# LayerNorm in a two-layer backbone: the norm's output from the centred residual in two VectorE operations a tile, the residual's own normalisation as a third one later, and the Newton step on VectorE

## The chip, the cores and the metric

The kernel runs on one core of one Trainium2 chip. The metric is the device time of one execution in microseconds (us). Before the change the median of three runs is 1936.71 us. A core has five engines that each work through a queue of their own in order: TensorE (PE, matrix products), VectorE (DVE), ScalarE (ACT), GpSimd (POOL) and SyncE (SP, which issues most transfers). They wait for each other by semaphores.

## The reference, cut to what matters

The reference is a backbone of two layers over 256 latent tokens and 256 context tokens, 1024 features each, in float32. Each layer has three sublayers: a SwiGLU, a mixer (an mLSTM in the first layer, windowed attention in the second) and another SwiGLU. Each is followed by a LayerNorm of the scaled residual, and its input is that residual, modulated by coefficients from a conditioning vector:

```python
def layer_norm(x, g, b):
    mu = xf.mean(-1, keepdims=True)
    var = jnp.mean(jnp.square(xf - mu), -1, keepdims=True)
    return ((xf - mu) * lax.rsqrt(var + LN_EPS) * g + b)

def modulate(s, m, slot):
    return s * (1 + m[..., 3 * slot + 1, :]) + m[..., 3 * slot, :]

def residual_post_norm(s, y, gate, weight, g, b):
    return layer_norm(ALPHA * s + weight * gate * y, g, b)
```

Between two sublayers the kernel needs two results of a norm: `u`, the modulated input of the next sublayer (soon), and `ALPHA` times the normalised residual, to which the next sublayer's output is added (late).

## The kernel before

The residual lies feature-major in eight tiles `as_[d]` of 128 features by 512 tokens. Columns `C0` (0 to 255) are the context, `C1` (256 to 511) the latent tokens. A matrix product in float32 is made of three products of halves: each operand is split into a rounded high part and a low part, the rest. Weights come by DMA into `raw` tiles; ScalarE writes the high part (L384), VectorE the low part as raw minus high (L385, L1298 for the attention's weights). One matmul of 128x128 by 256 columns follows the other at about 0.12 us.

A hand-written planner emits the program: tasks are generators with priorities, a clock `k.T` counts TensorE's time, and each `yield` says how much of that time is to pass before a task goes on. TensorE's and SyncE's orders are the planner's own; the orders of VectorE, ScalarE and GpSimd come from a scheduler with priorities.

`class Norm` makes one norm. There are five between the sublayers: into the mLSTM, after it, after the first layer's last SwiGLU, into attention, and after attention. The first four work on two halves, `C0` first and then `C1`; the fifth on `C1` alone (`solo`). (A sixth, `Last`, writes the output and is another class.) The steps of a norm:

- `__init__`: a per-token shift is taken off the residual on GpSimd (L88).
- `add`: when a sublayer's output `y` for tile d has been added (L787, VectorE, reads PSUM), sums of the residual and of its square are accumulated (L107, L108) on VectorE or GpSimd.
- `finish(cs)`, once for each half, nine times in all: small matmuls (`stat`) sum over the features. ScalarE squares the mean (L138) and copies the mean square plus `EPS` (L139), GpSimd subtracts (L140). `rsqrt` is a power on GpSimd (L820) and a Newton step of four operations on GpSimd (L822 to L825), all on 128x2 values `ln`. GpSimd then takes the mean off eight tiles (L145). Matmuls spread `rstd` over 128 partitions into a PSUM tile.
- Then, for each tile: VectorE multiplies the tile by `rstd` (L168), ScalarE makes the high part `uh` = tile x A + B (L581), VectorE the same in full as `uf` (L582) and the low part `ul` = `uf` - `uh` (L583). The solo norm writes both parts into one tile `up`. Head matmuls of the next sublayer (`xm`, `gv`, `k`, `v`) read `uh` and `ul` tile by tile.
- After a yield of `RY`, GpSimd scales the tile for the residual, times `ALPHA` g plus `ALPHA` b (L174).

Of the kernel before, what the change touches and what calls it, by code (L numbers as in the profile page):

```python
# [8 lines left out]
F32 = mybir.dt.float32  # L9
# [4 lines left out]
AF = mybir.ActivationFunctionType  # L14
ALU = mybir.AluOpType
# [7 lines left out]
EPS = 1e-5  # L23
# [49 lines left out]
class Norm:  # L73
# [44 lines left out]
    def finish(s, cs):  # L118
        k, nc = s.k, s.k.nc
        P = nc.gpsimd  # L120
        k.res[cs.start] = Ev()
        yield 0 if s.solo else LAT[0] if cs == s.halves[0] else LAT[1]

        st = k.ps("stat")
        o = 256 - cs.start
        parts = [(s.a1[:, cs], s.a2[:, cs])]
        if s.solo:

            parts.append((k.as_[KD - 1][:, cs], s.sq[:, cs]))
        for i, p in enumerate(parts):  # L130
            for n in range(2):
                s.moments(st, o, p[n], n, i == n == 0)
        for i, p in enumerate(parts):
            k.mm(st[:, cs], k.ones[1024], p[0], False, i == len(parts) - 1)
        mu = s.a1
        w = [k.sp.tile([128, 2], F32, tag=f"ln{n}", name="ln", bufs=2) for n in range(4)]
        with k.tc.high_priority(offset=400):
            nc.scalar.activation(w[0], st[:, o:o + 2], AF.Square)  # L138
            nc.scalar.activation(w[1], st[:, o + 2:o + 4], AF.Copy, bias=EPS)  # L139
            P.tensor_tensor(out=w[1], in0=w[1], in1=w[0], op=ALU.subtract)  # L140
            y = k.rsqrt(w[1], w[2], w[3], True)
        nc.scalar.activation(mu[:, cs], st[:, cs], AF.Copy)
        for d in range(KD):
            r = k.as_[d][:, cs]
            k.tc.keep_in_program_order(P.tensor_tensor(out=r, in0=r, in1=mu[:, cs], op=ALU.subtract))  # L145
        if s.solo:
            k.free(s.sq)
        s.left -= 1
        if s.left == 0:
            k.calm.t = k.T + CALM  # L150
        if s.left == 0:
            k.free(s.a1, s.a2)
        if s.solo:
            k.keep_warm(WARM[0])
        yield SOLO if s.solo else LAT[2]
        bc = k.ps("rstd")
        for t in range(2):
            k.mm(bc[:, cs.start + 128 * t:cs.start + 128 * t + 128], y[:, t:t + 1].to_broadcast([128, 128]), k.ident, t == 0, True)
        if s.solo:
            k.keep_warm(WARM[1])  # L160
        c = 0 if cs == C1 else 1
        s.ready[cs.start].t = k.T + (LAT[3] if cs == s.halves[0] else LAT[4])
        y = bc[:, cs]
        if s.u is None:
            s.u = k.new_u(s.solo)
        for d in range(KD):
            r = k.as_[d][:, cs]
            nc.vector.tensor_tensor(out=r, in0=r, in1=y, op=ALU.mult)  # L168
            A, B = s.AB
            k.modulate(r, A[:, d, c:c + 1], B[:, d, c:c + 1], cs, s.u[d])  # L170
        yield RY
        for d in range(KD):
            r = k.as_[d][:, cs]
            nc.gpsimd.tensor_scalar(out=r, in0=r, scalar1=s.ag[:, 0, d:d + 1], scalar2=s.ag[:, 1, d:d + 1], op0=ALU.mult, op1=ALU.add)  # L174
        k.res[cs.start].t = k.T


# [1405 lines left out]
```

## Time and profile before

| | |
|---|---|
| Runs, us | 1936.71, 1938.23, 1934.01 (median 1936.71) |
| The profiled execution, us | 1940.04, its span 1938.0 |
| Mean granted TensorE clock | 0.983 |
| TensorE busy | 1884.1 us, 97% of the span |
| VectorE busy | 1355.2 us, 70% |
| ScalarE busy | 835.0 us, 43% |
| GpSimd busy | 365.8 us, 19% |

The times in the profile's rows are from the start of the span. In a row, the first number is the start, the second the duration, then engine, line and operation, what it writes and reads, how many instructions the row merges, and in brackets how long the engine had been idle and what ended that. The busy share of TensorE says that most of the kernel cannot be moved by other engines; the places where TensorE waits for one are short and known by name. The clock in a stretch is the share of TensorE's full speed that was granted there.

### The profile page before, as it was taken

What the parts mean: (1) busy time and instruction counts of PE and PEld (TensorE: products, weight loads), DVE (VectorE), ACT (ScalarE), POOL (GpSimd) and SP (SyncE); (2) the same over time, 40 slices, a digit from 0 to 9 for tenths busy, and PEclk for the clock granted to TensorE, in tenths of its full rate; (3) what the DMA queues carried; (4) which work ended last, traced back from release to release, by engine and by line L of the source; (5) the groups of instructions that cost most, each with busy time, mean ns of one, the idle gap of its engine ahead of it and who ended that gap; (6) DMA issues with size and microseconds to landing.
All of it is one profiled execution on the core that took longest, in us unless ns stands there. A gap on an engine that the chain in (4) does not pass through costs nothing.

```text
span 1938.0 us, 28054 instructions
## 1 busy us (share of the span) xinstructions
PE 1884.1 (97%) x10498; PEld 1594.5 (82%) x10498; DVE 1355.2 (70%) x2476; ACT 835.0 (43%) x1565; POOL 365.8 (19%) x397
## 2 busy tenths in 40 slices
PE   7999999999999999989999999999999999989997
PEld 4888888897889977978888889888888898788887
DVE  4976677976664679767776679876733468967675
ACT  3443233246555563343323333433223335747562
POOL 2000000570012344450000015400000256130000
PEclk9999999999999999989999999999999999989999
DMA  9654454435343364325454444354422324125653
GB/s 317 218 202 167 152 192 161 136 121 184 96 150 115 129 220 141 109 93 185 153 200 174 158 136 142 127 199 152 153 89 91 103 73 131 45 66 172 210 174 98
DMA packets 227432, 287.49 MB, mean 148 GB/s; under 512 B 7968, under 2 KB 197536, under 8 KB 227296
## 3 DMA queue, kind: packets, MB, share of 16 engines
q1 hardware_dynamic: 226384, 282.75, 44.0%
q0 software_dynamic: 912, 2.95, 0.4%
q8 instruction: 82, 1.34, 0.3%
q14 instruction: 54, 0.44, 0.1%
HBM read 269.94 MB, written 15.73 MB: 147 GB/s over the span
## 4 chain that ended last, share of the span: by engine, by line
PE 56%; DVE 3%; POOL 1%; issue 1%; ACT 0%; DVEq 0%; POOLq 0%; ACTq 0%
PE gv L294 31%; PE y L294 19%; PE q L294 1%; PE o L294 1%; PE s L294 1%; DVE ul L583 1%; PE stat L294 1%; DVE uf L582 0%; PE pT L301 0%; PE msum L294 0%; PE h L294 0%; POOL as L145 0%; DVE as L168 0%; ACT e L1412 0%; PE swap L294 0%
## 5 line engine op out<-in xcount | busy, mean ns | idle before, releaser
L294 PE MATMUL gv<-uh,w 128*128 128x512 f32 (+1 forms) x2240 | 673.1, 381 | 11.0 <-DVE w L385 5.5
L384 ACT ACTIVATE w<-raw 128x512 fp32r<-128x512 f32 x636 | 395.9, 630 | 667.0 <-PE gv L294 373.8
L385 DVE TENSOR_TENSOR w<-raw,w 128x512 fp32r<-128x512 f32 x604 | 433.3, 724 | 278.5 <-ACT w L384 275.4
L294 PEld LDWEIGHTS gv<-uh,w 128*128 128x128 f32 x2240 | 417.3, 191 | 97.3 <-DVE w L385 5.7
L294 PE MATMUL gv<-ul,w 128*128 128x512 f32 (+1 forms) x1120 | 425.3, 380 | 0.1
L502 DVE SCALAR_TENSOR_TENSOR macc<-mraw,cs,macc 128x512 f32<-128x512 f32 x448 | 330.9, 784 | 44.4 <-DMA mraw<-in_mod_w 32.8
L294 PE MATMUL y<-hh,w 128*128 128x512 f32 (+1 forms) x1248 | 341.1, 359 | 0.0
L294 PEld LDWEIGHTS y<-hh,w 128*128 128x128 f32 x1248 | 222.6, 189 | 37.8 <-issue 3.2
L294 PEld LDWEIGHTS gv<-ul,w 128*128 128x128 f32 x1120 | 213.5, 191 | 38.6 <-DVE ul L583 0.6
L88 POOL TENSOR_TENSOR as<-as,shift 128x512 f32<-128x512 f32 (+1 forms) x40 | 57.6, 1475 | 889.6 <-ACT shift L86 889.6
L294 PE MATMUL y<-hl,w 128*128 128x512 f32 (+1 forms) x624 | 222.4, 356 | 0.0
L294 PEld LDWEIGHTS y<-hl,w 128*128 128x128 f32 x624 | 117.9, 189 | 17.5 <-issue 0.7
L294 PE MATMUL gv<-up,w 128*128 128x512 f32 x704 | 125.1, 340 | 2.0 <-DVE up L583 2.0
L294 PEld LDWEIGHTS gv<-up,w 128*128 128x128 f32 x704 | 109.8, 192 | 17.2 <-DVE up L583 2.3
L787 DVE SCALAR_TENSOR_TENSOR as<-y,gate,as 128x256 f32<-128x256 f32 x192 | 82.0, 476 | 34.6 <-PE y L294 34.5
L294 PE MATMUL z<-w,uh 128*128 128x256 f32 x512 | 94.1, 285 | 0.0
L294 PE MATMUL xm<-uh,w 128*128 128x512 f32 (+1 forms) x320 | 91.7, 360 | 0.0
L294 PE MATMUL y<-hnh,w 128*128 128x512 f32 (+1 forms) x320 | 85.2, 350 | 1.4 <-DVE as L787 1.4
L385 POOL TENSOR_TENSOR w<-raw,w 128x512 fp32r<-128x512 f32 x32 | 46.4, 1452 | 201.0 <-ACT w L384 194.5
L294 PEld LDWEIGHTS z<-w,uh 128*128 128x128 f32 x512 | 79.8, 191 | 2.5 <-issue 2.1
L700 DVE TENSOR_TENSOR sg<-sg,gv 128x512 f32<-128x512 f32 x66 | 44.9, 685 | 48.9 <-PE gv L294 47.5
L294 PE MATMUL z<-w,ul 128*128 128x256 f32 x256 | 72.4, 283 | 0.0
(309 smaller groups left out, 2541.3 us busy)
## 6 DMA issues: line engine op xcount, KB each, us to landing
raw<-in_ffn_w_in SPq DMA_DIRECT2D x84, 1024.0 KB, 5.2
mraw<-in_mod_w SPq DMA_DIRECT2D x128, 512.0 KB, 6.2
raw<-in_ffn_w_out SPq DMA_DIRECT2D x48, 768.0 KB, 4.6
raw<-in_ml_w_up SPq DMA_DIRECT2D x15, 1024.0 KB, 5.7
m<-in_mod_w SPq DMA_DIRECT2D x32, 256.0 KB, 6.6
raw<-in_ffn_w_out SPq DMA_DIRECT2D x16, 512.0 KB, 3.5
raw<-in_ml_w_down SPq DMA_DIRECT2D x16, 512.0 KB, 4.0
raw<-in_at_w_qkv SPq DMA_DIRECT2D x6, 1024.0 KB, 5.1
```

What stands on the lines that cost most here:

```text
L88: nc.gpsimd.tensor_tensor(out=k.as_[d][:, cols], in0=k.as_[d][:, cols], in1=sh[:, cols], op=ALU.subtract)
L294: k.nc.tensor.matmul(out, lhsT=lhsT, rhs=rhs, start=start, stop=stop, skip_group_check=True, **kw)
L384: k.nc.scalar.activation(h, view, AF.Copy)
L385: (k.nc.gpsimd if pool else k.nc.vector).tensor_tensor(out=l, in0=view, in1=h.bitcast(F32), op=ALU.subtract)
L502: V.scalar_tensor_tensor(out=o, in0=r, scalar=cf, in1=o, op0=ALU.mult, op1=ALU.add)
L583: nc.vector.tensor_tensor(out=lo, in0=f[:, cs], in1=hi.bitcast(F32), op=ALU.subtract)
L700: nc.vector.tensor_tensor(out=sg[:, cols], in0=sg[:, cols], in1=gv[1][:, cols], op=ALU.mult)
L787: nc.vector.scalar_tensor_tensor(out=k.as_[d][:, cs], in0=ys[dp][e][:, part], scalar=G[:, d, c:c + 1], in1=k.as_[d][:, cs], op0=ALU.mult, ...
```

## The change

The variance is now one VectorE operation from the statistics in PSUM and ScalarE's square (L141). The power stays on GpSimd (L143). The Newton step is three operations on VectorE (L144 to L146). The mean is still taken off on GpSimd (now L150). For each tile `uf` = tile x A x `rstd` is one VectorE operation that reads `rstd` in PSUM (L175), ScalarE adds B for the high part (L177), and VectorE makes the low part as (`uf` + B) - high (L178). `rstd` is copied to SBUF by ScalarE (L181). After the yield, VectorE multiplies the tile by that copy (L185) and GpSimd does what L174 did (now L186). VectorE has 36 instructions more, GpSimd 45 fewer, ScalarE as many as before; TensorE's and SyncE's orders are the same. Below `Norm`, lines move by 13: L385 becomes L398, L787 L800, L1298 L1311.

```diff
@@ -134,11 +134,16 @@
             k.mm(st[:, cs], k.ones[1024], p[0], False, i == len(parts) - 1)
         mu = s.a1
         w = [k.sp.tile([128, 2], F32, tag=f"ln{n}", name="ln", bufs=2) for n in range(4)]
+        V = nc.vector
         with k.tc.high_priority(offset=400):
+
             nc.scalar.activation(w[0], st[:, o:o + 2], AF.Square)
-            nc.scalar.activation(w[1], st[:, o + 2:o + 4], AF.Copy, bias=EPS)
-            P.tensor_tensor(out=w[1], in0=w[1], in1=w[0], op=ALU.subtract)
-            y = k.rsqrt(w[1], w[2], w[3], True)
+            V.scalar_tensor_tensor(out=w[1], in0=st[:, o + 2:o + 4], scalar=EPS, in1=w[0], op0=ALU.add, op1=ALU.subtract)
+            y, t = w[2], w[3]
+            P.tensor_tensor(out=y, in0=w[1], in1=k.mhalf[:, 0:2], op=ALU.pow)
+            V.scalar_tensor_tensor(out=t, in0=w[1], scalar=-0.5, in1=y, op0=ALU.mult, op1=ALU.mult)
+            V.tensor_tensor(out=t, in0=t, in1=y, op=ALU.mult)
+            V.scalar_tensor_tensor(out=y, in0=t, scalar=1.5, in1=y, op0=ALU.add, op1=ALU.mult)
         nc.scalar.activation(mu[:, cs], st[:, cs], AF.Copy)
         for d in range(KD):
             r = k.as_[d][:, cs]
@@ -160,18 +165,26 @@
             k.keep_warm(WARM[1])
         c = 0 if cs == C1 else 1
         s.ready[cs.start].t = k.T + (LAT[3] if cs == s.halves[0] else LAT[4])
-        y = bc[:, cs]
         if s.u is None:
             s.u = k.new_u(s.solo)
+        A, B = s.AB
         for d in range(KD):
-            r = k.as_[d][:, cs]
-            nc.vector.tensor_tensor(out=r, in0=r, in1=y, op=ALU.mult)
-            A, B = s.AB
-            k.modulate(r, A[:, d, c:c + 1], B[:, d, c:c + 1], cs, s.u[d])
+
+            f = k.a(name="uf")
+            bd = B[:, d, c:c + 1]
+            nc.vector.scalar_tensor_tensor(out=f[:, cs], in0=k.as_[d][:, cs], scalar=A[:, d, c:c + 1], in1=bc[:, cs], op0=ALU.mult, op1=ALU.mult)
+            hi, lo = k.hl(s.u[d], cs)
+            nc.scalar.activation(hi, f[:, cs], AF.Identity, bias=bd)
+            nc.vector.scalar_tensor_tensor(out=lo, in0=f[:, cs], scalar=bd, in1=hi.bitcast(F32), op0=ALU.add, op1=ALU.subtract)
+            k.free(f)
+        rs = k.a(name="rstd")
+        nc.scalar.activation(rs[:, cs], bc[:, cs], AF.Copy)
         yield RY
         for d in range(KD):
             r = k.as_[d][:, cs]
-            nc.gpsimd.tensor_scalar(out=r, in0=r, scalar1=s.ag[:, 0, d:d + 1], scalar2=s.ag[:, 1, d:d + 1], op0=ALU.mult, op1=ALU.add)
+            nc.vector.tensor_tensor(out=r, in0=r, in1=rs[:, cs], op=ALU.mult)
+            P.tensor_scalar(out=r, in0=r, scalar1=s.ag[:, 0, d:d + 1], scalar2=s.ag[:, 1, d:d + 1], op0=ALU.mult, op1=ALU.add)
+        k.free(rs)
         k.res[cs.start].t = k.T
 
 
```

The scheduler moves other instructions with these. Three places follow, all of them VectorE's queue. In the names, `as_` are residual tiles, `y_` a sublayer's output in PSUM, `w_` halves of weights, `acc1_` and `acc2_` the sums, `sq_` a squared tile.

First half of the norm into the mLSTM, before, from the end of the last sums to the first low part:

```order
L787 SCALAR_TENSOR_TENSOR as_120<-y_3204,gate00_1555,as_120 128x256
L787 SCALAR_TENSOR_TENSOR as_121<-y_3205,gate00_1555,as_121 128x256
L107 TENSOR_TENSOR acc1_2962<-acc1_2962,as_120 128x256
L385 TENSOR_TENSOR w_3458<-raw_3152,w_3457 128x512
L107 TENSOR_TENSOR acc1_2962<-acc1_2962,as_121 128x256
L385 TENSOR_TENSOR w_3547<-raw_3190,w_3546 128x512
L168 TENSOR_TENSOR as_116<-as_116,rstd_3469 128x256
L168 TENSOR_TENSOR as_117<-as_117,rstd_3469 128x256
L582 TENSOR_SCALAR uf_3489<-as_116,cBA_2955,cBB_2956 128x256
L582 TENSOR_SCALAR uf_3494<-as_117,cBA_2955,cBB_2956 128x256
L583 TENSOR_TENSOR ul0_3473<-uf_3489,uh0_3472 128x256
```

and now:

```order
L141 SCALAR_TENSOR_TENSOR ln_3395<-stat_3388,ln_3394 128x2
L144 SCALAR_TENSOR_TENSOR ln_3397<-ln_3395,ln_3396 128x2
L800 SCALAR_TENSOR_TENSOR as_120<-y_3204,gate00_1555,as_120 128x256
L145 TENSOR_TENSOR ln_3397<-ln_3397,ln_3396 128x2
L800 SCALAR_TENSOR_TENSOR as_121<-y_3205,gate00_1555,as_121 128x256
L146 SCALAR_TENSOR_TENSOR ln_3396<-ln_3397,ln_3396 128x2
L107 TENSOR_TENSOR acc1_2962<-acc1_2962,as_120 128x256
L398 TENSOR_TENSOR w_3456<-raw_3152,w_3455 128x512
L107 TENSOR_TENSOR acc1_2962<-acc1_2962,as_121 128x256
L398 TENSOR_TENSOR w_3539<-raw_3190,w_3538 128x512
L175 SCALAR_TENSOR_TENSOR uf_3486<-as_116,cBA_2955,rstd_3467 128x256
```

Variance and Newton step stand among the additions of `y` and ahead of the two sums and two splits that were there before.

First half of the norm after the mLSTM, before, from the last but one pair of additions:

```order
L787 SCALAR_TENSOR_TENSOR as_6650<-y_8114,gate01_6682,as_6650 128x256
L787 SCALAR_TENSOR_TENSOR as_6651<-y_8115,gate01_6682,as_6651 128x256
L107 TENSOR_TENSOR acc1_7511<-acc1_7511,as_6650 128x256
L385 TENSOR_TENSOR w_8141<-raw_7680,w_8140 128x512
L108 TENSOR_TENSOR acc2_7512<-acc2_7512,sq_8195 128x256
L107 TENSOR_TENSOR acc1_7511<-acc1_7511,as_6651 128x256
L108 TENSOR_TENSOR acc2_7512<-acc2_7512,sq_8200 128x256
L107 TENSOR_TENSOR acc1_7511<-acc1_7511,as_6652 128x256
L385 TENSOR_TENSOR w_8145<-raw_7680,w_8144 128x512
```

and now:

```order
L107 TENSOR_TENSOR acc1_7511<-acc1_7511,as_6652 128x256
L108 TENSOR_TENSOR acc2_7512<-acc2_7512,sq_8192 128x256
L107 TENSOR_TENSOR acc1_7511<-acc1_7511,as_6653 128x256
L185 TENSOR_TENSOR as_6647<-as_6647,rstd_8092 128x256
...
L185 TENSOR_TENSOR as_6653<-as_6653,rstd_8092 128x256
L398 TENSOR_TENSOR w_8137<-raw_7680,w_8136 128x512
L398 TENSOR_TENSOR w_8133<-raw_7680,w_8132 128x512
```

The split that TensorE waits for there (low part of `w_8141` before, `w_8133` now) stood between the first and the second of these sums and now stands behind all of them, the L185 and another split.

Second half of the norm into attention, before, up to its first tile:

```order
L1298 TENSOR_TENSOR w_14509<-raw_14122,w_14508 128x512
L1329 CAST bmask_14526<-ident_73 128x128
L385 TENSOR_TENSOR w_14475<-raw_14088,w_14474 128x512
L1298 TENSOR_TENSOR w_14815<-raw_14122,w_14814 128x512
L168 TENSOR_TENSOR as_6646<-as_6646,rstd_14638 128x256
L168 TENSOR_TENSOR as_6647<-as_6647,rstd_14638 128x256
```

and now:

```order
L144 SCALAR_TENSOR_TENSOR ln_14576<-ln_14574,ln_14575 128x2
L185 TENSOR_TENSOR as_6648<-as_6648,rstd_14434 128x256
L145 TENSOR_TENSOR ln_14576<-ln_14576,ln_14575 128x2
L185 TENSOR_TENSOR as_6649<-as_6649,rstd_14434 128x256
L146 SCALAR_TENSOR_TENSOR ln_14575<-ln_14576,ln_14575 128x2
L185 TENSOR_TENSOR as_6650<-as_6650,rstd_14434 128x256
...
L185 TENSOR_TENSOR as_6653<-as_6653,rstd_14434 128x256
L398 TENSOR_TENSOR w_14467<-raw_14088,w_14466 128x512
L1311 TENSOR_TENSOR w_14807<-raw_14122,w_14806 128x512
L175 SCALAR_TENSOR_TENSOR uf_14631<-as_6646,cAA_13911,rstd_14628 128x256
```

The split of `w_14475` (now `w_14467`), which the first `v` matmuls behind the second half's `rstd` read, stood ahead of the wait for that `rstd` and now stands behind the Newton step and eight L185.

## The prediction

> **What bounds the kernel now.** I read the page's busy times and its chain of waits first, then the stretches around the five norms for busy time and clock, then TensorE's waits there, and last VectorE and GpSimd row by row.
>
> ```profile
> PE 1884.1 (97%) x10498; PEld 1594.5 (82%) x10498; DVE 1355.2 (70%) x2476; ACT 835.0 (43%) x1565; POOL 365.8 (19%) x397
> PE 56%; DVE 3%; POOL 1%; issue 1%; ACT 0%; DVEq 0%; POOLq 0%; ACTq 0%
> ```
>
> TensorE is the bound, so the change can act only where TensorE waits for a norm. I call the norms N1 (into the mLSTM), N2 (after it), N3, N4 (into attention), all with two halves, and N5 (after attention, latent columns alone). One stretch each, with the engines' busy time and the granted clock:
>
> ```profile
> 392.00:418.00 26.00, 24.10 (x171) 23.38 (x170) 20.31 (x45) 10.71 (x25) 21.03 (x33) 0.87 0.40 123
> 812.00:848.00 36.00, 28.52 (x197) 27.73 (x196) 25.19 (x55) 13.93 (x32) 26.33 (x40) 0.81 0.18 59
> 1200.00:1226.00 26.00, 24.36 (x186) 23.79 (x185) 22.73 (x47) 12.24 (x28) 21.13 (x33) 0.93 0.25 82
> 1576.00:1622.00 46.00, 42.07 (x335) 40.57 (x334) 39.42 (x80) 23.89 (x50) 38.40 (x51) 1.00 0.25 77
> 1726.00:1752.00 26.00, 22.96 (x117) 20.24 (x116) 16.56 (x35) 10.49 (x24) 15.18 (x22) 0.74 0.13 42
> ```
>
> The order of the numbers is TensorE, its weight loads, VectorE, ScalarE, GpSimd (busy us), clock, DMA. All but N4 also pay a slow clock after their waits. The waits themselves stand in brackets, with what ended them:
>
> ```profile
> 408.58 1.67 PE L294 MATMUL stat<-ones,acc 128*128 128x1 f32 x8 [1.68 <-DVE acc L107]
> ...
> 416.87 0.60 PE L294 MATMUL rstd<-ident,ln 128*128 128x128 f32 x4
> ...
> 827.12 0.39 PE L294 MATMUL gv<-uh,w 128*128 128x256 f32 x1 [1.98 <-DVE as L787]
> ...
> 833.13 0.80 PE L294 MATMUL gv<-uh,w 128*128 128x256 f32 x2 [5.50 <-DVE w L385]
> ...
> 1216.50 1.26 PE L294 MATMUL stat<-ones,acc 128*128 128x1 f32 x8 [1.59 <-DVE acc L107]
> ...
> 1223.36 0.71 PE L294 MATMUL rstd<-ident,ln 128*128 128x128 f32 x4
> ...
> 1593.52 1.34 PE L294 MATMUL stat<-ones,acc 128*128 128x1 f32 x8 [1.23 <-DVE acc L107]
> 1601.58 0.71 PE L294 MATMUL rstd<-ident,ln 128*128 128x128 f32 x4 [1.88 <-POOL ln L825]
> 1605.42 0.38 PE L294 MATMUL k<-ul,w 128*128 128x256 f32 x1 [0.48 <-DVE ul L583]
> ...
> 1737.98 2.29 PE L294 MATMUL gv<-up,w 128*128 128x512 f32 x6 [1.97 <-DVE up L583]
> ```
>
> Nearly every wait ends on VectorE, which therefore sets these stretches; the change adds instructions to VectorE and takes them from GpSimd.
>
> **The price that decides: VectorE beside GpSimd.** A VectorE operation with two SBUF inputs is stopped by a running GpSimd TENSOR_TENSOR. The nearest relative of the new Newton steps (same formula, 128x4) shows it: it lasts 163 ns, or 1252.
>
> ```profile
> L827 DVE SCALAR_TENSOR_TENSOR rsn<-ve,rsn x4: 163/706/1252, 662.2 to 780.6; 128x4 f32<-128x4 f32 x4
> ```
> ```profile
> 662.22 1.25 DVE L827 SCALAR_TENSOR_TENSOR rsn<-ve,rsn 128x4 f32<-128x4 f32 x1 [1.16 <-POOL rsn L820]
> ```
> ```profile
> 662.17 1.28 POOL L385 TENSOR_TENSOR w<-raw,w 128x512 fp32r<-128x512 f32 x1
> ```
>
> It began 0.05 us after GpSimd's operation and ended with it. Full tiles do the same: two L583 beside the stream of L145 take 1.83 us, 0.92 each, against 0.41 alone or beside GpSimd's TENSOR_SCALAR (L174). Operations with an input in PSUM are never slowed (L787: 192 between 449 and 489 ns).
>
> ```profile
> 399.97 1.83 DVE L583 TENSOR_TENSOR ul<-uf,uh 128x256 fp32r<-128x256 f32 x2
> ```
> ```profile
> 394.09 0.73 POOL L820 TENSOR_TENSOR ln<-ln,mhalf 128x2 f32<-128x2 f32 x1
> ...
> 395.91 0.52 POOL L825 TENSOR_TENSOR ln<-ln 128x2 f32<-128x2 f32 x1
> 396.39 6.72 POOL L145 TENSOR_TENSOR as<-as,acc 128x256 f32<-128x256 f32 x8
> ```
> ```profile
> 1610.79 0.41 DVE L583 TENSOR_TENSOR ul<-uf,uh 128x256 fp32r<-128x256 f32 x1
> ```
> ```profile
> 1607.52 9.55 POOL L174 TENSOR_SCALAR as<-as,ag 128x256 f32<-128x256 f32 x8
> ```
> ```profile
> L787 DVE SCALAR_TENSOR_TENSOR as<-y,gate,as x192: 449/476/489, 181.5 to 1926.6; 128x256 f32<-128x256 f32 x192
> ```
>
> **The change, part by part.**
>
> *Variance (L138 to L140).* One ScalarE copy and one GpSimd subtraction become one VectorE operation with a PSUM input. pow starts about 0.15 us sooner (estimate from the 0.20 us subtraction and its handover). ScalarE's nine copies come back as the copies of rstd (L181); ScalarE is 43% busy, so I cost these at nothing.
>
> *Newton.* GpSimd spent 396.43 - 394.82 = 1.6 us on it in N1. On VectorE three operations would take 3 x 0.16 = 0.5 us free, but pow is now followed at once by the eight subtractions of the mean (L150, the old L145, about 0.6 us each between VectorE's turns). All three have two SBUF inputs, so each waits out one: 3 x 0.7 = 2.1 us. Bounds 0.5 and 2.3; I take 2.1, because L827 met exactly this neighbour after the same pow.
>
> *Per tile.* L168, L582 and L583 become L175 (PSUM input, 0.40, not stopped) and L178 (two SBUF inputs, 0.92 beside GpSimd's stream). That is 1.3 us instead of 0.33 + 0.58 + 0.92 = 1.8 in the stream, 0.73 instead of 1.06 out of it.
>
> *First halves of N1, N3, N4.* In N1 the rows that count are these:
>
> ```profile
> 395.36 0.41 DVE L107 TENSOR_TENSOR acc<-acc,as 128x256 f32<-128x256 f32 x1
> 395.69 0.69 DVE L385 TENSOR_TENSOR w<-raw,w 128x512 fp32r<-128x512 f32 x1
> 396.29 0.42 DVE L107 TENSOR_TENSOR acc<-acc,as 128x256 f32<-128x256 f32 x1
> 396.96 0.89 DVE L385 TENSOR_TENSOR w<-raw,w 128x512 fp32r<-128x512 f32 x1 [0.25 <-ACT w L384]
> ...
> 408.76 0.42 DVE L108 TENSOR_TENSOR acc<-acc,sq 128x256 f32<-128x256 f32 x1
> ```
> ```profile
> 402.36 0.28 PE L294 MATMUL xm<-uh,w 128*128 128x256 f32 x1
> 402.48 0.28 PE L294 MATMUL xm<-ul,w 128*128 128x256 f32 x1
> ```
>
> GpSimd's stream now starts 1.6 us sooner, onto two L107 and two splits that ran free before (2.4 us); they now take 2 x 0.93 + 2 x 1.2 = 4.3. From the end of pow: Newton 2.1, these 4.3, three L175 1.2, the first L178 0.35: 7.95 us, in N1 394.7 + 7.95 = 402.65. The second head matmul wants it at 402.48: 0.2 lost. The rest runs out of the stream and is shorter: L178 once more beside it 0.5, then 13 operations at 0.33 to 0.40, so the last sum for the second statistics is done 13.5 us after pow, at 408.2 instead of 408.76 + 0.42 = 409.2. About 0.9 gained in each.
>
> *Second halves of N1 and N3.* The eight late L185 (two SBUF inputs) stand between the Newton steps and ahead of the second half's L175. From the end of pow: three Newton steps and two L185 alternate with GpSimd, 3 x 0.7 + 2 x 0.93 = 4.0 to rstd; then three L185 at 0.93, three free at 0.33, a split 0.6, three L175 1.2, L178 0.35: the first low part after 9.9 us. In N3 the first pow ends at 1203.1, the sums at 1216.6; behind them L178, L175, two splits, L141 (2.1 us) and pow (0.7): 1219.4. So rstd comes at 1223.4, as before, but the low part at 1229.3. TensorE is due there 33 matmuls after rstd, at the 0.12 us from one to the next in the rows above: 1223.36 + 0.48 + 4.0 = 1227.8. +1.5. N1 has the same delays, but its 1.68 us wait has become one of about 1.1, which by N4's 1.23 (clock 1.00) should not slow the clock: its point comes at 420.9 instead of 416.87 + 0.48 + 4.0 = 421.3, -0.4.
>
> *N4.* After the sums (1593.3) VectorE has 3.1 us of work up to L141, then one L186 and pow: 1597.75. The Newton steps mostly meet L186, so 2.1 with two L185: rstd at 1599.9, not 1601.58. But the split of w_14467, which TensorE needs 0.8 us after rstd, now stands behind Newton and four more L185, beside L150.
>
> ```profile
> 1599.12 0.71 DVE L385 TENSOR_TENSOR w<-raw,w 128x512 fp32r<-128x512 f32 x1
> ```
>
> It was done at 1599.83. Now: 1599.8 + 4 x 0.93 + 1.2 = 1604.7, a wait of 4 us. The second half begins 18 matmuls (2.2) later; with 1.1 of slow clock (N3's stretch lost 0.07 x 26 = 1.8 after its wait, N1's 0.13 x 26 = 3.4) that is 1608.0 instead of 1605.42: +2.6. Free of contention, the split is done by 1601.7 and the loss is gone.
>
> The last eight L185 and L186 of N4 must end before the residual's next shift:
>
> ```profile
> 1618.55 0.59 PE L294 MATMUL shift<-as,ones 128*128 128x256 f32 x2
> ```
>
> From 1612.3 on they and three splits take VectorE 4.6 us, GpSimd one L186 more, to about 1618: in time, the shift itself being 2.6 later. In the other norms the head matmuls of the second half (8 x 1.4 us) cover them. The two small transfers on GpSimd's queue in N4 now stand behind all of L150, at much the same time, 28 us ahead of their use.
>
> *N2.* The split that ends the 5.50 us wait stood ahead of the second moment sums:
>
> ```profile
> 832.39 0.68 DVE L385 TENSOR_TENSOR w<-raw,w 128x512 fp32r<-128x512 f32 x1
> ```
>
> Now it stands behind all four sums of each kind, eight L185 and another split. The first wait (bank freed by L787, now L800) ends 0.9 later, because Newton moves rstd from 817.6 to 818.65. From the second L800, at 828.35: 5.2 us to the last sum, seven L185 beside TENSOR_SCALAR 2.3, two splits 1.2: 837.1 instead of 833.1, +4.0. Behind it fewer matmuls fall into slow clock (0.19 x 36 = 6.8 us were lost in this stretch); I take back 1.0. +3.0, bounds +1.0 (the L185 find gaps among the sums) and +4.5.
>
> *N5.*
>
> ```profile
> 1731.63 0.71 POOL L820 TENSOR_TENSOR ln<-ln,mhalf 128x2 f32<-128x2 f32 x1
> ```
> ```profile
> 1736.99 1.81 DVE L583 TENSOR_TENSOR up<-uf,up 128x256 fp32r<-128x256 f32 x2
> ```
>
> Nothing stands between the Newton steps here: 2.1 instead of 1.1 us, pow 0.15 sooner, rstd +0.9. From rstd to the first low part the old chain took 4.4 us (TensorE waits until 1737.98); three L175 and one L178 behind 1.3 us of matmul take 2.9 to 3.5. Between -0.6 and 0; I take -0.3.
>
> Sum: -0.4 + 3.0 + 1.5 + 2.6 - 0.3 = +6.4 us. Against the profiled 1940.04 that is 1946.4; the median lies 3.3 below that execution, so 1943.1.
>
> **Rivals.** (1) Faster: the small steps slip in between GpSimd's operations, and L178 and L185 mostly miss the stream. It decides where rstd comes within 1.2 us of pow. N1's wait falls to about 0.4 and its slow clock goes (1.3 + 3.4 + 0.2 = -4.9), N3 likewise (1.2 + 1.7 = -2.9), N4 loses its waits of 1.23, 1.88 and 0.48 (-3.5), N5 gains 0.5 at rstd and 1.5 behind it (-2.0), N2 keeps the late split (+2.4): -10.9, so 1925.8. The L827 of 163 ns speaks for it, but there GpSimd stood idle after pow. (2) The parts cancel: Newton is stopped, but the L185 hold up nothing, as GpSimd's stream is through in time: N1 -2, N2 +1, N3 and N4 0, N5 -0.5: -1.5, so 1935.2. For it speaks that TensorE takes 4 us from rstd to the second half; against it, that L185 stands ahead of L175 on VectorE and that N4's split has only 0.8 us. (3) L186, though a TENSOR_SCALAR, stops VectorE too, by the 0.92 - 0.41 = 0.5 us that L145 costs L583: seven L185 in N2, 3.6 more, 1946.7. L583 at 0.41 beside L174 speaks against it.
>
> The Trainium skill, "SBUF — State Buffer", section "SBUF: two separate sides", states (3) as a rule: a VectorE operation with two SBUF inputs and any GpSimd operation that reads SBUF exclude each other for a whole instruction. The rows agree with it for TENSOR_TENSOR and not for TENSOR_SCALAR, so the sum above goes by the rows.
>
> **How the numbers follow.** Forecast 0.45, (1) 0.20, (2) 0.27, (3) 0.08. Below 0.2% (3.9 us) a measurement tells no change: slower 0.53, same 0.27, faster 0.20. The range, 1931 to 1949, leaves out most of (1); above it ends where N2 takes its upper bound and N1 keeps its slow clock (+1.5 + 1.9 + 2). The forecast's own range is 1940 to 1949.
>
> **What would show it.** Right: L144 to L146 at 0.6 to 0.8 us beside L150, L175 at 0.45; a new TensorE wait of 2 us or more for a split in N4, right after rstd; N2's second wait ending on L398 at 7 us or more; statistics waits in N1 and N3 shorter. Wrong: Newton steps near 0.16 us, or L185 at 0.41 throughout; then (1) or (2).

## The result, and the profile after

The changed kernel takes 1958.49 us (median of four, 1951.6 to 1960.01) against 1935.36 before (four, 1933.41 to 1938.23): a ratio of 1.0116, interval 1.0100 to 1.0133. That is 23 us slower. The profiled execution took 1958.88 us, its span 1957.1, at a clock of 0.984. So the span pair differs by 19.1 us; the execution profiled before lay 4.7 above its median. Executions in a second, slower state, which a few of the experiments below met, are left out of the medians given here.

The page after, busy times and the chain of waits:

```profile
PE 1885.3 (96%) x10498; PEld 1592.4 (81%) x10498; DVE 1376.0 (70%) x2512; ACT 827.7 (42%) x1565; POOL 364.7 (19%) x352
PE 55%; DVE 5%; issue 1%; ACT 0%; POOL 0%; DVEq 0%; ACTq 0%; POOLq 0%
```

TensorE is busy 1.2 us more in a span 19 us longer, and the chain has 5% of VectorE instead of 3%: the time went into waits. TensorE's order is the same, so each of its instructions can be set against itself. Its start after, less its start before, is called its delay here; where the delay grows, time was lost. These are rows of TensorE's timeline after (in brackets the wait and what ended it):

```profile
406.63 0.61 PE L307 MATMUL stat<-ones,acc 128*128 128x1 f32 x4 [0.51 <-DVE acc L107]
...
420.40 0.39 PE L307 MATMUL xm<-ul,w 128*128 128x256 f32 x1 [0.38 <-DVE ul L178]
...
439.09 2.94 PE L307 MATMUL v<-bv,xm 128*128 128x128 f32 x24 [0.93 <-DVE xm L1025]
445.47 0.50 PE L307 MATMUL q<-xch,bm 128*128 128x512 f32 x1 [1.36 <-ACT xch L581]
446.71 0.50 PE L307 MATMUL q<-xcl,bm 128*128 128x512 f32 x1 [0.75 <-DVE xcl L582]
...
456.33 0.58 PE L307 MATMUL S<-xch,ql 128*128 128x256 f32 x1 [3.35 <-DVE ql L582]
...
835.51 0.39 PE L307 MATMUL gv<-uh,w 128*128 128x256 f32 x1 [1.33 <-DVE as L800]
846.54 0.79 PE L307 MATMUL gv<-uh,w 128*128 128x256 f32 x2 [10.52 <-DVE w L398]
...
1233.83 0.71 PE L307 MATMUL rstd<-ident,ln 128*128 128x128 f32 x4 [0.90 <-DVE ln L146]
1240.08 0.38 PE L307 MATMUL gv<-uh,w 128*128 128x256 f32 x1 [1.59 <-ACT uh L177]
...
1614.45 0.71 PE L307 MATMUL rstd<-ident,ln 128*128 128x128 f32 x4 [1.31 <-DVE ln L146]
1618.52 0.58 PE L307 MATMUL v<-w,uh 128*128 128x256 f32 x1 [2.88 <-DVE w L398]
...
1656.25 0.50 PE L307 MATMUL s<-rph 64*128 64x512 f32 x2 [1.56 <-ACT rph L581]
...
1751.38 0.71 PE L307 MATMUL rstd<-ident,ln 128*128 128x128 f32 x4 [2.42 <-DVE ln L146]
1754.38 2.08 PE L307 MATMUL gv<-up,w 128*128 128x512 f32 x5 [1.62 <-DVE up L178]
```

The delay ahead of each place and behind it, with what ran at a slow clock after its waits:

| place | delay ahead, behind | lost | forecast |
|---|---|---|---|
| N1 (390 to 430) | -0.5, 0.6 | 1.1 | -0.4 |
| start of the mLSTM (430 to 470) | 0.6, 7.9 | 7.3 | none |
| N2 (812 to 860) | 8.7, 11.6 | 2.9 | 3.0 |
| N3 (1200 to 1250) | 11.6, 14.4 | 2.9 | 1.5 |
| N4 (1590 to 1630) | 14.4, 16.9 | 2.5 | 2.6 |
| start of the attention (1650 to 1670) | 16.9, 19.0 | 2.1 | none |
| N5 (1740 to 1760) | 17.4, 16.3 | -1.1 | -0.3 |

Between these places the delay grows by 0.8 in the rest of the mLSTM and falls by 1.6 in the rest of the attention, mostly where TensorE's clock was 0.50 before (1703 to 1706) and is 1.00 now. Over the last SwiGLU it grows by 2.9; there TensorE has no wait in either kernel, and the same stretch takes 189 or 192 us in executions of different kernels, so no edit is read from that. The five norms together lost 8.3 us, not far from the 6.4 forecast. The largest single loss lies at a place where the prediction had nothing, the start of the mLSTM. The wait at 446.71, for instance, stood at 443.54 before and was half as long:

```profile
443.54 0.51 PE L294 MATMUL q<-xcl,bm 128*128 128x512 f32 x1 [0.37 <-DVE xcl L569]
```

VectorE and GpSimd there, after:

```profile
426.09 2.76 DVE L185 TENSOR_TENSOR as<-as,rstd 128x256 f32<-128x256 f32 x8
428.78 3.09 DVE L398 TENSOR_TENSOR w<-raw,w 128x512 fp32r<-128x512 f32 x5
431.79 0.68 DVE L927 TENSOR_TENSOR bm<-mqkl,cst 128x512 fp32r<-128x512 f32 x1
432.39 0.68 DVE L927 TENSOR_TENSOR bv<-par,cst 128x512 f32<-128x512 f32 x1
...
438.27 0.17 DVE L92 TENSOR_SCALAR ag<-par 128x8 f32<-128x8 f32 x1 [4.00 <-POOL as L186]
438.35 1.88 DVE L1025 COPY xm<-xm 128x512 f32<-128x512 f32 x3
```
```profile
426.61 6.89 POOL L186 TENSOR_SCALAR as<-as,ag 128x256 f32<-128x256 f32 x1 [2.88 <-DVE as L185]
433.79 0.63 POOL L968 DMA_DIRECT2D rs<-as  x1 [0.30 <-POOL as L186]
434.47 3.77 POOL L186 TENSOR_SCALAR as<-as,ag 128x256 f32<-128x256 f32 x7
438.19 3.79 POOL L968 DMA_DIRECT2D rs<-as  x7
```

One late scaling of GpSimd, which takes 0.54 us in the next row (3.77 for seven), lasts 6.89 us. It begins 0.5 us into an unbroken run of fifteen VectorE operations with two SBUF inputs (eight L185, five splits, two L927, until 433.07) and ends 0.4 us behind that run. VectorE pays nothing: its eight L185 run at 0.345 us. Then seven scalings are still to come; L92, which resets the coefficients `ag` that they read, waits 4.00 us for the last; and the copies of `xm` that `v` needs stand behind L92 on VectorE. Before, the same places read:

```profile
428.32 3.25 POOL L174 TENSOR_SCALAR as<-as,ag 128x256 f32<-128x256 f32 x2
```
```profile
433.82 0.25 DVE L92 TENSOR_SCALAR ag<-par 128x8 f32<-128x8 f32 x2 [1.72 <-POOL as L174]
```

GpSimd was held up there before too, but less: two scalings took 3.25 us. The late multiplications made the VectorE run longer and left all eight scalings to it or to the time behind it.

Late in N4 GpSimd is held up again. Its last eight scalings, the first of them 5.08 us long, keep it until 1637.7, and a product of the attention (`kf`), for which it stood idle before, follows only then (after, then before):

```profile
1628.43 9.32 POOL L186 TENSOR_SCALAR as<-as,ag 128x256 f32<-128x256 f32 x8 [4.37 <-DVE as L185]
1637.72 1.44 POOL L1328 TENSOR_TENSOR kf<-kf,rope 128x256 f32<-128x256 f32 x2
```
```profile
1618.31 1.43 POOL L1315 TENSOR_TENSOR kf<-kf,rope 128x256 f32<-128x256 f32 x2 [1.24 <-PE swap L294]
```

How TensorE's wait of 1.56 us at 1656.25 comes about is not shown by this: it is gone in two runs below whose scalings end only about 1 us sooner, set against TensorE.

### The profile page after: what moved, and what is told of

The parts are those of the page before. It is cut to its first block, busy times and chain, and to the rows that moved or that the text cites. A ratio compares the mean times of both kernels' runs of the same rounds, so it can differ in the third digit from the quotient of the medians.

```text
span 1957.1 us, 27898 instructions
## 1 busy us (share of the span) xinstructions
PE 1885.3 (96%) x10498; PEld 1592.4 (81%) x10498; DVE 1376.0 (70%) x2512; ACT 827.7 (42%) x1565; POOL 364.7 (19%) x352
## 4 chain that ended last, share of the span: by engine, by line
PE 55%; DVE 5%; issue 1%; ACT 0%; POOL 0%; DVEq 0%; ACTq 0%; POOLq 0%
PE gv L307 31%; PE y L307 19%; PE s L307 1%; PE q L307 1%; DVE w L398 1%; DVE uf L175 1%; DVE as L185 1%; DVE ul L178 1%; PE o L307 1%; PE pT L314 0%; PE msum L307 0%; PE v L307 0%; PE h L307 0%; PE stat L307 0%; PE k L307 0%
## 5 line engine op out<-in xcount | busy, mean ns | idle before, releaser
L398 DVE TENSOR_TENSOR w<-raw,w 128x512 fp32r<-128x512 f32 x604 | 437.6, 731 | 275.8 <-ACT w L397 272.9
L800 DVE SCALAR_TENSOR_TENSOR as<-y,gate,as 128x256 f32<-128x256 f32 x192 | 82.2, 474 | 29.4 <-PE y L307 29.4
L398 POOL TENSOR_TENSOR w<-raw,w 128x512 fp32r<-128x512 f32 x32 | 46.5, 1454 | 200.6 <-ACT w L397 192.5
L186 POOL TENSOR_SCALAR as<-as,ag 128x256 f32<-128x256 f32 x72 | 68.5, 963 | 32.3 <-DVE as L185 25.6
```

The lines of the kernel that those rows point to most:

```text
L186: P.tensor_scalar(out=r, in0=r, scalar1=s.ag[:, 0, d:d + 1], scalar2=s.ag[:, 1, d:d + 1], op0=ALU.mult, op1=ALU.add)
L398: (k.nc.gpsimd if pool else k.nc.vector).tensor_tensor(out=l, in0=view, in1=h.bitcast(F32), op=ALU.subtract)
L800: nc.vector.scalar_tensor_tensor(out=k.as_[d][:, cs], in0=ys[dp][e][:, part], scalar=G[:, d, c:c + 1], in1=k.as_[d][:, cs], op0=ALU.mult, ...
```

## Experiments

Each was timed in five rounds beside the kernel before, whose median was 1934.9 to 1937.1 in them. The intervals of the ratios are 2 to 3.6 us to each side.

### The change in parts

**Newton step back on GpSimd**, the rest as changed.

```diff
-            y, t = w[2], w[3]
-            P.tensor_tensor(out=y, in0=w[1], in1=k.mhalf[:, 0:2], op=ALU.pow)
-            V.scalar_tensor_tensor(...)   # and the two others
+            y = k.rsqrt(w[1], w[2], w[3], True)
```

> The changed kernel with the Newton step back on GpSimd as four operations; variance, tile part and late multiplication as changed. Theory A (the late multiplications L185 in VectorE's queue cost most): the Newton step is worth 0.5 to 1 us where rstd ends a wait (N3 0.90, N4 1.31, N5 2.42), so 3 to 5 us faster than the changed kernel, 1953 to 1956 us. Theory B (the Newton step, stopped by GpSimd's stream, costs most): nearly all of the loss goes, 1936 to 1942 us.

1945.27 us, ratio 1.0051 (1.0033 to 1.0069): 13.2 less than the whole change, between the two theories. The start of the mLSTM still loses 6.7 us instead of 7.3. No single scaling lasts as long as VectorE's run here, but nine take 11.03 us beside it and L92 waits 4.25 us for the seven behind them:

```profile
422.76 11.03 POOL L182 TENSOR_SCALAR as<-as,ag 128x256 f32<-128x256 f32 x9
```

N4's wait for the split and the one at the attention are gone. The two profiled spans differ by 10.1 us: 2.6 came in at the start of the attention, 2.7 in the last SwiGLU, from which no edit is read, and the rest in steps of one to two microseconds.

**Variance and Newton step alone** on the kernel before.

> The kernel before with only the variance and the Newton step moved to VectorE; three operations a tile ahead of the yield as before, no late multiplication. Theory A: slower than before by 1 to 4 us (rstd about 1 us later in N5 and N2, less elsewhere), 1937 to 1940 us. Theory B: slower by 12 us or more, 1948 us and up.

1941.15 us, ratio 1.0029 (1.0019 to 1.0040): +5.5 against the kernel before in the same rounds, over the 1 to 4 expected, though the interval (3.7 to 7.7) touches it. The two parts alone add up to some 15, not to 23.

**Late multiplication on GpSimd.**

```diff
-            nc.vector.tensor_tensor(out=r, in0=r, in1=rs[:, cs], op=ALU.mult)
+            P.tensor_tensor(out=r, in0=r, in1=rs[:, cs], op=ALU.mult)
```

> The changed kernel with the late multiplication L185 on GpSimd in place of VectorE. Theory A: the splits in N2 and N4 are reached 2 to 4 us sooner each and the start of the mLSTM too: 6 to 12 us faster than the changed kernel, 1946 to 1952 us, less if GpSimd, which now takes about 1.35 us for each late tile, stores the residual later before the mLSTM. Theory B: within 2 us of the changed kernel, 1956 to 1960 us.

1977.0 us, ratio 1.0211 (1.0192 to 1.0229): 18.5 slower than the change, a clear miss. Against before, the profiled execution loses 12.5 us at the start of the mLSTM and 18 in N4. There the second half's power (L143) now stands behind the first half's late work on GpSimd's queue, and then the Newton step's first operation on VectorE takes 6.82 us beside more of that work and the mean subtraction (TensorE, GpSimd, VectorE):

```profile
1633.62 1.23 PE L307 MATMUL rstd<-ident,ln 128*128 128x128 f32 x4 [12.51 <-DVE ln L146]
```
```profile
1617.29 1.78 POOL L185 TENSOR_TENSOR as<-as,rstd 128x256 f32<-128x256 f32 x2 [5.34 <-ACT ln L140]
...
1623.52 0.72 POOL L143 TENSOR_TENSOR ln<-ln,mhalf 128x2 f32<-128x2 f32 x1
```
```profile
1624.27 6.82 DVE L144 SCALAR_TENSOR_TENSOR ln<-ln 128x2 f32<-128x2 f32 x1 [3.60 <-POOL ln L143]
```

### The start of the mLSTM

**Five buffers for `ag`** (`bufs=2` becomes `bufs=5`), so that L92 waits for no scaling; first on the changed kernel, then on the one before.

> The changed kernel with five buffers for ag (ALPHA times g and b) in place of two, so that L92 for a later norm need not wait for the late L186 of an earlier one. In the changed kernel VectorE stands 4.00 us at L92 before the mLSTM, until GpSimd's L186 are done. Theory A with that wait as the cause of the loss at the start of the mLSTM (about 7 us between 436 and 459 us): 4 to 7 us faster than the changed kernel, 1951 to 1954 us. Rival (the late stores of the residual and the transfers behind them cause it): 0 to 1 us faster.

1953.49 us, ratio 1.0087 (1.0069 to 1.0105): 5.0 less than the change, and the start of the mLSTM loses 3.6 us instead of 7.3. The wait at `v` is gone. A scaling of 6.90 us is still there, and so is a wait of 2.69 for `ql`, the low part of the mLSTM's q: the buffer was the path of a part of the loss, not its cause.

> The kernel before with five buffers for ag and nothing else. VectorE stood 1.72 us at L92 before the mLSTM. If that wait reached TensorE (its gaps there are 0.41, 0.37 and 0.29 us): up to 1 us faster, 1934.5 to 1935.7 us, which a measurement will hardly tell from no change.

1935.71 us, ratio 1.0002 (0.9990 to 1.0014): before, L92's 1.72 us held up nothing that shows in these rounds.

**Late multiplications last in VectorE's priority.**

```diff
-            nc.vector.tensor_tensor(out=r, in0=r, in1=rs[:, cs], op=ALU.mult)
+            with k.tc.high_priority(offset=-400):
+                nc.vector.tensor_tensor(out=r, in0=r, in1=rs[:, cs], op=ALU.mult)
```

> The changed kernel with only the scheduler's priority of the late multiplication lowered (by 400), so that in N4 the split of w_14467 and in N2 the split that TensorE waits for come ahead of the eight L185; Newton step on VectorE as changed. Theory A (the place of L185 in VectorE's queue is the loss): the 2.88 us wait of N4 goes, N2's 10.52 falls to about 7: 5 to 9 us faster than the changed kernel, 1949 to 1954 us. Theory C (Newton on VectorE lets GpSimd's stream start 1.5 to 2 us sooner and this stream, not the order, slows everything behind it): within 2 us, 1956 to 1960 us.

1963.1 us, ratio 1.0143 (1.0127 to 1.0160): 4.6 over the change, with intervals that just overlap, and in any case not faster, a miss. N2's wait for the split fell from 10.52 to 6.91 and N4's went. But N2's second half got a wait of 3.62 us for `rstd`, the multiplications now came later, and at the start of the mLSTM GpSimd was shut out for longer, 8.14 us in one scaling (GpSimd, VectorE, TensorE; lines are one higher here):

```profile
424.37 12.49 POOL L187 TENSOR_SCALAR as<-as,ag 128x256 f32<-128x256 f32 x8 [3.86 <-DVE as L186]
```
```profile
441.64 0.17 DVE L92 TENSOR_SCALAR ag<-par 128x8 f32<-128x8 f32 x1 [8.28 <-POOL as L187]
```
```profile
442.46 1.86 PE L308 MATMUL v<-bv,xm 128*128 128x128 f32 x7 [6.18 <-DVE xm L1026]
```

**Newton step on GpSimd, five `ag`, late multiplications last**, together.

> The changed kernel with the Newton step on GpSimd, five buffers for ag and the late multiplication at low priority: the three mends together, of the change only the variance, the tile in two operations and the late multiplication on VectorE are left. If the parts add up: 1945.3 (Newton on GpSimd) - 5 (ag) - 3 to - 4 (N2's split sooner) = 1936 to 1938 us, level with the kernel before. If they repair the same waits: 1941 to 1945 us.

1942.35 us, ratio 1.0028 (1.0016 to 1.0041): the gains do not add up, which was the second expectation, and this version does not reach the kernel before.

**Late scaling on ScalarE**, the rest as changed. This takes GpSimd's TENSOR_SCALAR away and leaves every VectorE instruction.

```diff
-            P.tensor_scalar(out=r, in0=r, scalar1=s.ag[:, 0, d:d + 1], scalar2=s.ag[:, 1, d:d + 1], op0=ALU.mult, op1=ALU.add)
+            nc.scalar.activation(r, r, AF.Identity, bias=s.ag[:, 1, d:d + 1], scale=s.ag[:, 0, d:d + 1])
```

> The changed kernel with the late scaling (times ALPHA g plus ALPHA b, L186) on ScalarE in place of GpSimd. GpSimd's one L186 of 6.89 us before the mLSTM ran while VectorE issued two-input operations without a pause. Theory D (VectorE shuts GpSimd out there, and ag, the residual's stores and the mLSTM wait for that): the scaling is done by about 430 us, the waits at 439 to 456 us (6.4 us) shrink to 2 or less: 4 to 7 us faster than the changed kernel, 1951 to 1955 us, less what ScalarE's 0.6 us operations delay. Rival: those waits come from the number of operations on VectorE alone: within 1.5 us, 1957 to 1960 us.

1942.95 us, ratio 1.0040 (1.0027 to 1.0053): 15.5 less, far more than expected. VectorE runs the same L185, and L92 no longer waits (before: 1.72, changed: 4.00):

```profile
426.70 2.76 DVE L185 TENSOR_TENSOR as<-as,rstd 128x256 f32<-128x256 f32 x8
429.38 1.28 DVE L398 TENSOR_TENSOR w<-raw,w 128x512 fp32r<-128x512 f32 x2
430.58 0.68 DVE L927 TENSOR_TENSOR bv<-par,cst 128x512 f32<-128x512 f32 x1
431.23 0.25 DVE L92 TENSOR_SCALAR ag<-par 128x8 f32<-128x8 f32 x2
```

The view of this tile by line, from 415 to 440 us, has ScalarE's scaling at 588 ns with next to no spread:

```profile
L186 ACT ACTIVATE as<-as,ag x13: 586/588/604, 415.2 to 430.6; 128x256 f32<-128x256 f32 x13
```

Nothing is left of the loss at the start of the mLSTM, and the wait at the attention is gone. N2's wait stays, at 9.93.

### The corners that were missing

The same edit of the late scaling, with the other parts.

> The changed kernel with the late scaling as a ScalarE activation (as in the run that gave 1942.95) and with the Newton step on GpSimd as before; the input in two VectorE operations and the late multiplication on VectorE stay. Theory C (the Newton step costs what it cost alone, 5.5 us, because its three small operations stand among GpSimd's two-input operations on VectorE): 1936 to 1938.5, within 0.2% of the kernel before. Theory D2 (the Newton step's cost beside the other parts came only through GpSimd's late scaling, which is gone here): 1941 to 1944, no better than with the Newton step on VectorE. If the two-operation input also gains what the prediction's first rival priced (about 10 us over the second halves), 1928 to 1934.

> The kernel before with one edit: the late scaling as a ScalarE activation instead of a GpSimd TENSOR_SCALAR. If GpSimd's late scaling was shut out by VectorE in the kernel before too, at a cost on TensorE's path (the reset of ag waited 1.72 us for it, the block of residual stores stands behind it): 1932 to 1935. If there it was covered, as the 0.0 us of waiting at the head of the mLSTM says: 1935 to 1938, within 0.2%.

> The kernel before with the variance and the Newton step on VectorE and the late scaling on ScalarE; the input in three operations, no late multiplication. If the Newton step costs 5.5 us by its own place on VectorE whatever GpSimd does (it cost 5.5 with the scaling on GpSimd and 5.6 beside the two-operation input with the scaling on ScalarE): 1928.6 + 5.5 = 1933 to 1936. If part of its cost alone came through GpSimd's late scaling starting sooner under VectorE's operations: 1929 to 1932.

The first took 1937.32 us (ratio 1.0005, 0.9993 to 1.0016), as the Newton step's own price had it. The second, the kernel before with this edit alone, took 1928.61 (0.9962, 0.9948 to 0.9976), better than either expectation: GpSimd's scaling did cost TensorE something before, in small pieces at N1, the start of the mLSTM, N3, N4 and N5. The third took 1934.4 (0.9999, 0.9987 to 1.0012), in the first expectation. With the other runs the eight combinations are (medians in us, each good to 2 to 3.6; the variance as one operation stands in every row but the first, and by itself shows no price in a run below):

| | late scaling on GpSimd | on ScalarE |
|---|---|---|
| three operations, Newton step on GpSimd | 1935.4 (before) | 1928.6 |
| three operations, Newton step on VectorE | 1941.2 | 1934.4 |
| two operations and late multiplication, Newton on GpSimd | 1945.3 | 1937.3 |
| two operations and late multiplication, Newton on VectorE | 1958.5 (after) | 1943.0 |

With the scaling on ScalarE the parts add: the Newton step 5.8 or 5.6, the two-operation input with its multiplication 8.7 or 8.6. With it on GpSimd they don't: 5.8 or 13.2, 9.9 or 17.3. So some 7.5 us of the 23 need all three together, and 7 us were there to be had without the change. The 7.5 is a difference of four such medians: that it is there is clear, its size is good to about 5.

### What the two-operation input is worth

**No late multiplication**, the rest as in the run of 1937.32. This kernel leaves out the late multiplications and the copy of `rstd` that they read (L181), so its residual is not normalised.

> The kernel that gave 1937.32 (input in two VectorE operations, Newton step on GpSimd, late scaling on ScalarE) without the late multiplications and the copy of the reciprocal deviation that they read: the residual stays unnormalised, so this leaves out part of the computation. If the two-operation input gains by itself what the prediction's first rival priced (some 10 us before what the late multiplications take) and these cost the rest: 1919 to 1926, clearly under the 1928.6 of the kernel with three operations and the scaling on ScalarE. If taking one VectorE operation in three off the input brings nothing, as the waits that end on the mean subtraction of GpSimd and on the weight halves suggest: 1927 to 1932.

1920.0 us, ratio 0.9916 (0.9899 to 0.9934). Against 1928.6 the two-operation input by itself gains 8.6; against 1937.3 the late multiplications with that copy cost 17.3. Then the two halves apart, on the best kernel so far, which itself is the kernel before with the scaling on ScalarE and the variance in one operation:

> The kernel before with the late scaling on ScalarE (the run that gave 1928.61) and one part of the change more: the variance as one VectorE operation instead of a ScalarE copy and a GpSimd subtraction; the Newton step stays on GpSimd, the input stays in three operations. If the shorter chain to the power operation counts (the waits for rstd that are left are 1.30 and 1.59 us, of which the prediction's 0.15 to 0.5 us each could go): 1926 to 1929. If the small operation stands behind longer ones on VectorE, as the Newton operations did alone: 1929 to 1933.

1928.5 us, ratio 0.9952 (0.9935 to 0.9968): not to be told from 1928.6.

> The kernel that gave 1928.50 (three operations, variance in one VectorE operation, Newton step on GpSimd, late scaling on ScalarE) with the input in two operations and the late multiplication in the second halves of the norms alone. If the gain of 8.6 us lies in the second halves (whose waits end on the input and on the weight halves behind it) and the late multiplications are dear mainly in the first halves, where they stand ahead of the second half's input: 1921 to 1927. If the second halves' own late multiplications, under the following matmuls, cost as much: 1928 to 1934.

> The same with the input in two operations and the late multiplication in the first halves alone. If the first halves' late multiplications stand ahead of the second halves' input and weight halves and that is where the 17.3 us are: 1932 to 1940. If they are hidden there: 1926 to 1930.

Second halves alone: 1928.58 (0.9966, 0.9954 to 0.9979), no difference from 1928.5. That is the second expectation: what their input gains, their own late multiplications take. First halves alone: 1937.14 (1.0008, 0.9998 to 1.0019), all of the 8.6. Both leave N5 in three operations. Set against the run of 1928.5, the profiled execution with the first halves loses 6.3 us at N2, 2.3 at N1, 2.1 in the mLSTM and about 1 each at N3 and N4. TensorE's rows at N2 show one place of it, first with the edit in the second halves, then in the first:

```profile
829.92 0.80 PE L309 MATMUL gv<-uh,w 128*128 128x256 f32 x2 [5.05 <-DVE w L400]
```
```profile
837.25 0.80 PE L309 MATMUL gv<-uh,w 128*128 128x256 f32 x2 [9.92 <-DVE w L400]
```

A first half's multiplications stand ahead of the weight splits and of the second half's input on VectorE. With the Newton step on GpSimd, as here, they also hold up GpSimd's power for the second half: it takes 4.0 to 4.2 us beside them in N1, N3 and N4, and at most 0.83 where the edit is in the second halves. N1's, with the edit in the first halves:

```profile
411.10 4.17 POOL L835 TENSOR_TENSOR ln<-ln,mhalf 128x2 f32<-128x2 f32 x1 [6.91 <-DVE ln L139]
```

> The kernel that gave 1937.32 (input in two VectorE operations, late multiplication on VectorE, Newton step on GpSimd, late scaling on ScalarE) with the late multiplications put last in the scheduler's priority, so that the weight halves for N2's second half (wait 9.93 us, against 5.35 where the input took three operations) pass them. If what is left of the loss is only the late multiplications' place in VectorE's queue: 1930 to 1934. If they are as dear in another place (after the second half's input, ahead of the projections' evictions): 1936 to 1940.

1937.45 us, ratio 0.9999 (0.9987 to 1.0010), the second expectation. In the profiled execution N2's wait fell from 9.93 to 6.91; N2 gained 5.3 us, the start of the mLSTM lost 2.4, and the span fell from 1937.9 to 1935.0. The medians, of twelve runs and of eleven, are the same; what cancels the rest in the other runs is not shown. No version with the two-operation input beat the kernel with three operations and the scaling on ScalarE.

## Why the prediction was wrong

The sign and most named places were right; the size was not: +6.4 forecast, +23 measured, outside the range.

- *Price of the Newton steps, 0.7 us beside the mean subtraction.* Right. The rows at N1's second half show VectorE's small steps and L185 in turn:

```profile
410.73 0.69 DVE L144 SCALAR_TENSOR_TENSOR ln<-ln 128x2 f32<-128x2 f32 x1 [0.60 <-POOL ln L143]
411.34 0.41 DVE L185 TENSOR_TENSOR as<-as,rstd 128x256 f32<-128x256 f32 x1
411.68 0.69 DVE L145 TENSOR_TENSOR ln<-ln 128x2 f32<-128x2 f32 x1
412.30 0.41 DVE L185 TENSOR_TENSOR as<-as,rstd 128x256 f32<-128x256 f32 x1
412.63 0.69 DVE L146 SCALAR_TENSOR_TENSOR ln<-ln 128x2 f32<-128x2 f32 x1
413.24 4.80 DVE L185 TENSOR_TENSOR as<-as,rstd 128x256 f32<-128x256 f32 x6
```

- *L175 never stopped.* Right (all between 464 and 482 ns in the view by line).
- *N1.* The statistics wait shrank, to 0.51 and 0.46 us. The second half's first low part was read at 420.40, 421.38 before: 0.5 sooner when the 0.5 ahead of N1 is taken off, against 0.4 forecast. That N1 still loses 1.1 is the slow clock behind this, 0.50 for 3.4 us after the waits of 1.27 and 0.38 at the input, which the sum did not price. The prediction also had it that a statistics wait of about 1.1 would not slow the clock; behind these two it was 0.50 for 3.4 us. (In N3 it stayed at 1.00 behind two waits of the same size, so the rows give no rule for it.)
- *N2.* Right in size and place: 2.9 against 3.0, and the wait named L398, at 10.52 (7 or more). The working behind it was right too: seven L185 (2.6 us) stand ahead of the splits. In part two errors cancel: the split came 0.7 later than forecast, and 1.8 came back behind it, not 1.0.

```profile
842.46 2.62 DVE L185 TENSOR_TENSOR as<-as,rstd 128x256 f32<-128x256 f32 x7
845.00 3.48 DVE L398 TENSOR_TENSOR w<-raw,w 128x512 fp32r<-128x512 f32 x5
```

- *N3.* The low part was read 1.3 later, against 1.5. The rest of the 2.9 is the clock, 0.50 for 3.4 us behind the input's wait of 1.59, which the sum did not price.
- *N4.* Right in sum, 2.5 against 2.6, and in place: rstd came 1.6 sooner (1.7 forecast). The wait for the split was named at 4 us and measured 2.88, and the slow clock behind it took 1.6, not 1.1, so here too errors cancel.
- *N5.* -1.1 against -0.3, beyond its bounds: rstd came 0.5 later, not 0.9. From rstd to the first low part it took 3.0 us (2.9 to 3.5 forecast).
- *The step that failed:* "In the other norms the head matmuls of the second half (8 x 1.4 us) cover them." In N1 they cover the late multiplications, which VectorE had done by 428.85. They do not cover the late scalings behind these: GpSimd was still at them at 438.2, and the mLSTM waited. This place cost 7.3 us and the attention's start 2.1; without GpSimd's scaling both losses are gone, though at the attention's start the path to TensorE stays open.
- *Why it failed:* of VectorE beside GpSimd's TENSOR_SCALAR I priced VectorE's side alone (0.41 us, nothing) and called the pair free. The price stood on the other side, and in a row that the prediction itself quotes: eight L174 in 9.55 us, 1.2 each, where one takes 0.55. Rival (3) looked for a loss of VectorE there and was rightly small; the loser is GpSimd. The rule of the Trainium skill that stood with it ("SBUF — State Buffer", section "SBUF: two separate sides") has the two exclude each other; what I took for disagreement was its other half. The scaling of 6.89 us agrees with it. The runs show who loses, which decides here.
- *Rival (1),* 10.9 us of gain, was half true: the two-operation input by itself gains 8.6. With the late multiplications the second halves come out even and the first halves cost 8.6.
- *What a sum over places could not see:* 7.5 us come only when Newton step, late multiplication and GpSimd's scaling are there together. Which wait carries them was not settled: with the Newton step back on GpSimd the delay shrinks by 1.2 us up to the end of the mLSTM's start, by some 5 in small steps from there to N4, and by 2.6 at the start of the attention.

Also open: the wait of 3.35 for `ql` at 456.33 goes back to VectorE waiting 3.60 us for a transfer to land (0.26 before). It is gone without GpSimd's scaling. The residual's stores (L968), issued late and all together, fit as the reason: from 436 to 452 us their queue moved 2.10 MB, against 0.49 before and 0.55 with the scaling on ScalarE, and the median of the four transfers (`xs`) was 6.9 us to landing, against 3.5 and 4.2. No run moved these stores alone, so this is argued and not shown.

## What to carry to other kernels

Price a pair of engines from both sides: an operation that runs at full speed beside another may be the one that shuts the other out. When work is added late to a queue, follow it to its last consumer, including the buffers that it releases and the reset that waits for them, and not only to the next TensorE wait. And a shorter critical input is worth little if the work put off is queued ahead of the next urgent thing: here the first halves lost 8.6 us so, and the second halves only came out even. The useful edit was another one: the late scaling on ScalarE, which was busy 43% of the time, for 0.4%.

## What the runs showed of the hardware

- A GpSimd TENSOR_SCALAR (128x256, 0.55 us) that started inside an unbroken run of VectorE operations with two SBUF inputs lasted until the run ended in the changed kernel, 6.89 us, and much the same with five `ag`, 6.90. With the multiplications last one lasted 8.14. VectorE's operations kept 0.345 us each. It is not always so: with the Newton step back on GpSimd nine scalings took 1.2 us each beside such a run, and VectorE's eight 0.395. What decides between the two is not shown.
- The power on GpSimd, a TENSOR_TENSOR of 128x2 that takes 0.71 us, took 4.17 beside eight late multiplications.
- With GpSimd's TENSOR_TENSOR the two mostly take turns (0.69 for a step of 0.16). But a Newton step of 128x2 took 6.82 us with the late multiplication on GpSimd, and once, with the multiplications last, it waited through all eight mean subtractions (VectorE, then GpSimd):

```profile
852.49 5.50 DVE L144 SCALAR_TENSOR_TENSOR ln<-ln 128x2 f32<-128x2 f32 x1 [1.65 <-POOL ln L143]
858.02 0.16 DVE L145 TENSOR_TENSOR ln<-ln 128x2 f32<-128x2 f32 x1
```
```profile
852.42 5.54 POOL L150 TENSOR_TENSOR as<-as,acc 128x256 f32<-128x256 f32 x8
```

So taking turns is no bound: the price of such a step lay between 0.16 and 6.82 us, and 0.7 was only its usual value.
